# A hybrid attention layer on one core: the first loads on two queues, the first weight split and the table load moved forward, the loads of the first phase pinned in order, the causal mask made on chip

## The chip, the core and the metric

The kernel runs on one core of a Trainium2 chip. The metric is device microseconds of one execution, the median of several runs. A core has a matrix engine (TensorE; PE in the profile, with its weight loads as PEld), a vector engine (VectorE, DVE), an activation engine (ScalarE, ACT), a general engine (GpSimd, POOL) and a queue engine (SyncE, SP) that in this kernel issues the DMA transfers. All tensors lie in the chip's memory when the kernel starts, and the output is written back there.

## The reference, cut to what matters

One decoder layer over 512 tokens of width 1024, all in float32:

```
h    = rms_norm(x, g_norm)
proj = h @ w_in                      # one wide projection, split into head groups
o_nsa  = nsa(q, kv, gate)            # 8 heads, 2 kv heads: compressed, selected and window attention
o_pool = pool(v_p);  o_mem = cross_attention(q_m, mem)
y   = concat(o_nsa*silu(z_n), o_pool*silu(z_p), o_mem*silu(z_m))
out = x + y @ w_out
```

At 512 tokens all 8 selection blocks of 64 are selected, so the selected branch and the window branch are plain causal attention with different keys and values, and both need the same causal mask. The compressed branch first turns keys and values, in blocks of 32 tokens, into 31 compressed ones with a small network (w_cmp1, w_cmp2).

## The kernel before

Every float32 product is made in three passes on the matrix engine: each operand is split into a rounded part `hi` and a rest `lo`, and hi·hi, hi·lo and lo·hi are added up in PSUM (`mm3`, lines 333 to 339). So each weight chunk goes through the same steps: a DMA into a tile `wr` (3 buffers; lines 152 and 428/429), a copy into `wh` on ACT (`split_w`, line 158), a subtraction into `wl` (line 161, on DVE or POOL), and then the matmuls.

The first phase is the projection of x onto the keys and values of the selected and window branches (called kv here). x comes transposed, in 8 chunks `xt[k]` of 128 columns of the model width (256 KB each, line 170). The weight comes in five pieces, with 1, 1, 2, 2 and 2 chunks (256 or 512 KB each, line 152). `split_gained` (lines 327 to 331) multiplies a chunk of x by the norm's gain (`g_col`, loaded at line 165) and splits it into `act_hi` (ACT, line 330) and `act_lo` (DVE, line 331). Then come 12 matmuls for each chunk: three passes for four row tiles (line 792), 96 in all. Ahead of them run `WU` = 14 warm-up matmuls on zeros (line 177).

The factor 1/rms of the rows is applied after the projection. For it the rows of x are loaded a second time, not transposed (512 KB for each of 4 row tiles, line 799), after the constants `cst` (line 796) and the positions; `row_square` sums their squares on ACT (line 309), `row_factors` makes the factors on DVE (lines 198 to 208 and 316 to 318), and `rows_to_columns` transposes them on PE (line 324) and copies them to `rstd_t` (ACT, line 325).

Then comes a list of steps, `EARLY`, in an order written out by hand: `W_kc` loads and splits the weight of the compressed branch (two chunks of 512 KB), `ci` multiplies by it (48 matmuls into two PSUM tiles, lines 337 to 339) and scales the result by `rstd_t` (DVE, line 464), `kv0` to `kv3` finish the kv row tiles (from line 393 on), `W_g`, `W_m`, `W_q` load and split the next weights, and so on; `LATE` is a second such list. The engines' own order of instructions isn't that of the program text: a planner orders each engine's stream with a timing model, and an instruction that is "kept in program order" is held behind the one traced just before it on the same engine.

The causal mask is part of `cst`: 512 columns, 384 of zeros and 128 with the triangle. `cst` has 534 KB.

Of the kernel before, what the change touches and what calls it, by code (L numbers as in the profile page):

```python
# [20 lines left out]
T = 512  # L21
# [20 lines left out]
CST_MASK = 0  # L42
CST_CMP = 512
# [8 lines left out]
def shape_constants():  # L52
    c = np.zeros((128, CST_GAIN), np.float32)
    p = np.arange(128)
    c[:, CST_MASK + 384:CST_MASK + 512] = np.where(p[None, :] <= p[:, None], 0.0, NEG)
# [12 lines left out]
    return c  # L68
# [23 lines left out]
EARLY = "W_kc kv0 kv1 kv2 W_g kv0 ci kv1 kv3 ms mr kv3 g2 g0 g0 kv2 g1 cm g1 g3 cm W_m g2 m0 m1 W_q g3 q1 cm q1 q3 m1 q0 q2 m0 q0"  # L92
LATE = "f rg rq q2 u u q3 u u f u f f u u u f c u f u u c u f u u u f f f u u u c u u u u u u c f u u u u u u u u u u f u u u u u u f"
WU = 14
# [3 lines left out]
def layer(ctx: ExitStack, tc: tile.TileContext, x, x_t, mem, mem_t, positions, g_cols, w_in, w_cmp1, w_cmp2, cmp_pos,  # L98
# [26 lines left out]
    def ps_out():  # L125
        return pp.tile([128, 512], F32, name="pO", bufs=1)
# [19 lines left out]

    def lo_eng(spec, i):
        return nc.gpsimd if spec and spec[i % len(spec)] == "p" else nc.vector

    def load_w(src, r0, kk, c0, width, name="wr", tag=None):  # L150
        wt = wp.tile([128, kk, width], F32, name="wr", bufs=3)
        nc.sync.dma_start(wt, src[r0:r0 + kk * 128, c0:c0 + width].rearrange("(k p) e -> p k e", p=128))
        return wt

    def split_w(wt, eng=None, pin=False, dst=None):
        shape = list(wt.shape)
        hi, lo = dst or (wp.tile(shape, F32R, name=name, bufs=4) for name in ("wh", "wl"))
        i = nc.scalar.activation(hi, wt, AF.Copy)  # L158
        if pin:
            tc.keep_in_program_order(i)  # L160
        (eng or nc.vector).tensor_sub(lo, wt, hi.bitcast(F32))  # L161
        return hi, lo

    g_col = cp.tile([128, 2, KT], F32, name="g_col")
    nc.sync.dma_start(g_col, g_cols)
    xt, kv_raw = [e8([128, 4, T]) for _ in range(2)], []
    xt = [xt[k // 4][:, k % 4] for k in range(KT)]
    for k0, kk in ((0, 1), (1, 1), (2, 2), (4, 2), (6, 2)):
        for k in range(k0, k0 + kk):
            nc.sync.dma_start(xt[k], x_t[:, k])  # L170
        kv_raw.append((k0, kk, load_w(w_in, k0 * 128, kk, C_KV, 512)))

    zeros = w2k([128, 256], BF16)
    nc.vector.memset(zeros, 0.0)
    warm = ps_out()
# [6 lines left out]
    nc.vector.tensor_copy(ident_r, ident)  # L182

# [136 lines left out]
    def rows_to_columns():  # L320

        pt = ps_t()
        for t in range(NT):
            nc.tensor.transpose(pt[:, t * 128:t * 128 + 128], row_rstd[:, 0, t:t + 1].to_broadcast([128, 128]), ident)
        nc.scalar.activation(rstd_t, pt, AF.Copy)
# [7 lines left out]
    def mm3(ps, pairs):  # L333

        n = len(pairs)
        for i, (sh, sl, mh, ml) in enumerate(pairs):
            nc.tensor.matmul(ps, sh, mh, start=(i == 0), stop=False)  # L337
            nc.tensor.matmul(ps, sh, ml, start=False, stop=False)  # L338
            nc.tensor.matmul(ps, sl, mh, start=False, stop=(i == n - 1))  # L339
# [20 lines left out]
    def proj_cols(ps, parts, c0):  # L360
# [5 lines left out]
        mm3(ps, pairs)  # L366
# [219 lines left out]
    def nsa_unit(pts, t, g, h, rr):  # L586
# [13 lines left out]
        p = softmax_pair(pv, n, cs[:, CST_MASK + 512 - n:CST_MASK + 512], q_nr[:, t, h:h + 1], gate[:, t, h, 1:3])  # L600
# [230 lines left out]
    def memory_rows_step():  # L831
# [7 lines left out]
        "W_kc": load_step("kc", lambda: chunk(w_in, C_KC, 256, 4, eng=LO["kc"])),  # L839
# [126 lines left out]
```

## Time and profile before

| what | value |
|---|---|
| median of 3 runs | 301.29 us (301.27 to 301.32) |
| the profiled execution, device time | 302.29 us |
| its span, first to last instruction | 300.5 us |
| PE busy | 283.7 us, 94% of the span |
| DVE, ACT, POOL busy | 72%, 57%, 14% |
| DMA moved | 30.5 MB |

The profile is of one execution. Its device time has 1.8 us outside its span, and it is 1.0 us above the median of the runs, which are not profiled. "Busy" counts instructions in flight; matmuls overlap, so the pace of a run of matmuls is read from their start times and not from their durations.

### The profile page before, as it was taken

What the parts mean: (1) busy time and instruction counts of PE and PEld (TensorE: products, weight loads), DVE (VectorE), ACT (ScalarE), POOL (GpSimd) and SP (SyncE); (2) the same over time, 40 slices, a digit from 0 to 9 for tenths busy, and PEclk for the clock granted to TensorE, in tenths of its full rate; (3) what the DMA queues carried; (4) which work ended last, traced back from release to release, by engine and by line L of the source; (5) the groups of instructions that cost most, each with busy time, mean ns of one, the idle gap of its engine ahead of it and who ended that gap; (6) DMA issues with size and microseconds to landing.
All of it is one profiled execution on the core that took longest, in us unless ns stands there. A gap on an engine that the chain in (4) does not pass through costs nothing.

```text
span 300.5 us, 4794 instructions
## 1 busy us (share of the span) xinstructions
PE 283.7 (94%) x1630; PEld 228.0 (76%) x1630; DVE 215.8 (72%) x653; ACT 172.4 (57%) x408; POOL 43.2 (14%) x67
## 2 busy tenths in 40 slices
PE   4999799989997999999999999869999999999995
PEld 3788589968875888888787888448768777877785
DVE  1674689899547986679888699997878788752221
ACT  4563743586712665778694738674687588743000
POOL 1010131312010830000000823330000000200000
PEclk9999999999998999999999999997999999999999
DMA  6999271283620082055022050720200200120031
GB/s 197 383 410 367 63 233 51 71 274 110 188 77 2 1 212 70 2 140 143 0 69 73 0 141 2 211 69 0 73 0 0 72 0 3 70 73 0 0 142 70
DMA packets 21897, 30.51 MB, mean 102 GB/s; under 512 B 2928, under 2 KB 12528, under 8 KB 21744
## 3 DMA queue, kind: packets, MB, share of 16 engines
q1 hardware_dynamic: 21872, 30.20, 31.9%
q8 instruction: 13, 0.21, 0.3%
q14 instruction: 12, 0.10, 0.1%
HBM read 28.10 MB, written 2.10 MB: 100 GB/s over the span
## 4 chain that ended last, share of the span: by engine, by line
PE 84%; DVE 9%; ACT 4%; issue 1%; DMA 1%; SPq 0%; ACTq 0%
PE pS L339 9%; PE pS L337 9%; PE pS L338 9%; PE pS L792 8%; PE pJ L339 7%; PE pJ L337 7%; PE pJ L338 7%; PE pO L621 6%; PE pT L604 5%; PE pS L598 3%; PE pT L388 2%; DVE w L536 2%; PE pS L658 1%; ACT w L538 1%; DVE w L553 1%; PE pS L471 1%
## 5 line engine op out<-in xcount | busy, mean ns | idle before, releaser
L538 ACT ACTIVATE w<-w,sm_st 128x128 f32<-128x128 f32 (+3 forms) x64 | 35.4, 555 | 9.5 <-DVE sm_st L536 9.0
L161 DVE TENSOR_TENSOR wl<-wr,wh 128x1024 fp32r<-128x1024 f32 (+3 forms) x26 | 30.4, 1169 | 10.1 <-ACT wh L158 9.9
L536 DVE CUSTOM_DVE_ANT_0 w<-pS,cst,q_nr 128x128 f32<-128x128 f32 (+3 forms) x64 | 32.6, 545 | 6.6 <-PE pT L604 5.6
L158 ACT ACTIVATE wh<-wr 128x1024 fp32r<-128x1024 f32 (+3 forms) x31 | 31.3, 1009 | 8.1 <-DMA wr<-in_w_in 6.2
L605 ACT ACTIVATE pt<-pT 128x128 f32<-128x128 f32 (+3 forms) x64 | 25.5, 429 | 18.1 <-PE pT L604 17.7
L337 PE MATMUL pS<-wh,act_hi 128*128 128x512 f32 (+2 forms) x94 | 33.8, 363 | 1.2 <-DVE w L262 1.2
L339 PE MATMUL pS<-wh,act_lo 128*128 128x512 f32 (+2 forms) x94 | 33.9, 362 | 0.0
L338 PE MATMUL pS<-wl,act_hi 128*128 128x512 f32 (+2 forms) x94 | 33.6, 361 | 0.0
L337 PE MATMUL pJ<-act_hi,wh 128*128 128x512 f32 x72 | 28.8, 399 | 1.8 <-ACT wh L158 1.8
L339 PE MATMUL pJ<-act_hi,wl 128*128 128x512 f32 x72 | 28.7, 398 | 0.1
L338 PE MATMUL pJ<-act_lo,wh 128*128 128x512 f32 x72 | 28.6, 397 | 0.0
L604 PE MATMUL pT<-ident,w 128*128 128x128 f32 x160 | 25.6, 277 | 1.5 <-ACT pt L605 0.8
L604 PEld LDWEIGHTS pT<-ident,w 128*128 128x128 f32 x160 | 19.2, 140 | 8.3 <-ACT pt L605 2.5
L553 DVE TENSOR_SCALAR w<-w,sm_st 128x256 f32<-128x256 f32 (+2 forms) x64 | 24.7, 425 | 0.9
L161 POOL TENSOR_TENSOR wl<-wr,wh 128x1024 fp32r<-128x1024 f32 x5 | 12.0, 2399 | 82.3 <-ACT wh L158 70.5
L337 PEld LDWEIGHTS pS<-wh,act_hi 128*128 128x128 f32 x94 | 18.1, 193 | 4.0 <-DVE w L262 1.3
L338 PEld LDWEIGHTS pS<-wl,act_hi 128*128 128x128 f32 x94 | 18.1, 193 | 2.4
L339 PEld LDWEIGHTS pS<-wh,act_lo 128*128 128x128 f32 x94 | 18.0, 191 | 2.4
L621 PE MATMUL pO<-pt,v_sw 128*64 128x256 f32 x160 | 19.0, 384 | 0.0
L337 PEld LDWEIGHTS pJ<-act_hi,wh 128*128 128x128 f32 x72 | 13.6, 189 | 4.4 <-ACT wh L158 2.0
L339 PEld LDWEIGHTS pJ<-act_hi,wl 128*128 128x128 f32 x72 | 13.5, 188 | 3.2 <-DVE wl L161 0.5
L338 PEld LDWEIGHTS pJ<-act_lo,wh 128*128 128x128 f32 x72 | 13.5, 188 | 2.6
(249 smaller groups left out, 631.4 us busy)
## 6 DMA issues: line engine op xcount, KB each, us to landing
wr<-in_w_in SPq DMA_DIRECT2D x15, 512.0 KB, 5.2
wr<-in_w_in SPq DMA_DIRECT2D x11, 256.0 KB, 3.8
e<-in_x_t SPq DMA_DIRECT2D x8, 256.0 KB, 7.5
e<-in_x SPq DMA_DIRECT2D x4, 512.0 KB, 8.0
wr<-in_w_mem_kv SPq DMA_DIRECT2D x4, 512.0 KB, 4.1
wr<-in_w_out SPq DMA_DIRECT2D x4, 512.0 KB, 4.0
wr<-in_w_out SPq DMA_DIRECT2D x8, 256.0 KB, 3.9
w<-in_x SPq DMA_DIRECT2D x8, 256.0 KB, 3.1
```

Of the source, the lines that this page charges most:

```text
L158: i = nc.scalar.activation(hi, wt, AF.Copy)
L161: (eng or nc.vector).tensor_sub(lo, wt, hi.bitcast(F32))
L337: nc.tensor.matmul(ps, sh, mh, start=(i == 0), stop=False)
L338: nc.tensor.matmul(ps, sh, ml, start=False, stop=False)
L339: nc.tensor.matmul(ps, sl, mh, start=False, stop=(i == n - 1))
L536: nc.vector.tensor_tensor_reduce(p[:, b, :n], ps[b], mask, r, 3e38, OP.add, OP.min, st[:, 0, b:b + 1])
L538: nc.scalar.activation(p[:, b, :n], p[:, b, :n], AF.Exp, bias=st[:, 0, b:b + 1], scale=-1.0, accum_out=st[:, 1, b:b + 1])
L553: nc.vector.tensor_scalar(p[:, b, :n], p[:, b, :n], st[:, 2, b:b + 1], None, op0=OP.mult)
L604: nc.tensor.transpose(pt[:, kt * 128:kt * 128 + 128], p[:, b, kt * 128:kt * 128 + 128], ident)
L605: nc.scalar.activation(pts[b][:, :, g, rr, :], pt[:, 0:n].rearrange("p (k q) -> p k q", k=t + 1), AF.Copy)
L621: m = nc.tensor.matmul(dst, v, p, start=(rp == 0 and i < 2), stop=(rp == 1 and i >= len(calls) - 2), skip_group_check=True)
L792: nc.tensor.matmul(kv_ps[t], a[:, k, t * 128:(t + 1) * 128], b[:, j], start=(k == 0 and b is wh and a is act_hi), stop=(k == KT - 1 and a ...
```

## The change

It moves and adds these things:

- The first weight piece and then `g_col` are issued from ACT's DMA queue; all other loads stay on SP, and SP begins with the first chunk of x.
- The loads of the first phase (x, weights, `W_kc`, `cst`, positions, rows of x, the compression weights, the memory rows) are kept in program order.
- A copy of one column of zeros on ACT is traced ahead of the first real ACT work, so the load of ACT's table comes with it.
- `wh` of the first weight piece is made by a copy on DVE.
- `WU` goes from 14 to 19.
- The two chunks of `W_kc` are loaded right after the kv weights, ahead of `cst` and the rows of x. The first is split after the kv splits, the second after the row sums.
- In `EARLY`, `ci` stands right behind `W_kc`; the first matmul of each of its two groups is kept in program order, and `rows_to_columns` is done between the two groups.
- The mask is made by POOL (a memset of 512 columns and one affine select on 128), and `cst` loses 512 columns (256 KB).

```diff
-EARLY = "W_kc kv0 kv1 kv2 W_g kv0 ci kv1 kv3 ms mr ...
+EARLY = "W_kc ci kv0 kv1 kv2 W_g kv0 kv1 kv3 ms mr ...
-WU = 14
+WU = 19
...
-    def split_w(wt, eng=None, pin=False, dst=None):
+    def split_w(wt, eng=None, pin=False, dst=None, hi_eng=None):
...
+        if hi_eng is not None:
+            hi_eng.tensor_copy(hi, wt)
+        else:
+            i = nc.scalar.activation(hi, wt, AF.Copy)
+            if pin:
+                tc.keep_in_program_order(i)
         (eng or nc.vector).tensor_sub(lo, wt, hi.bitcast(F32))
...
     g_col = cp.tile([128, 2, KT], F32, name="g_col")
-    nc.sync.dma_start(g_col, g_cols)
...
         for k in range(k0, k0 + kk):
-            nc.sync.dma_start(xt[k], x_t[:, k])
-        kv_raw.append((k0, kk, load_w(w_in, k0 * 128, kk, C_KV, 512)))
+            pinned(nc.sync.dma_start(xt[k], x_t[:, k]))
+        if k0 == 0:
+            wt = wp.tile([128, 1, 512], F32, name="wr", bufs=3)
+            nc.scalar.dma_start(wt, w_in[0:128, C_KV:C_KV + 512].rearrange("(k p) e -> p k e", p=128))
+            nc.scalar.dma_start(g_col, g_cols)
+        else:
+            wt = load_w(w_in, k0 * 128, kk, C_KV, 512, pin=True)
+        kv_raw.append((k0, kk, wt))
...
     nc.vector.memset(zeros, 0.0)
+    nc.scalar.activation(kp.tile([128, 1], F32, name="act0", bufs=1), zeros[:, 0:1], AF.Copy)
...
+    causal = cp.tile([128, T], F32, name="causal")
+    nc.gpsimd.memset(causal, 0.0)
+    nc.gpsimd.affine_select(out=causal[:, T - 128:], in_=causal[:, T - 128:], pattern=[[-1, 128]],
+                            compare_op=OP.is_ge, fill=NEG, base=0, channel_multiplier=1)
...
     def compress_in(kv2, parts):
         for i in range(2):
             ps = ps_early()
-            proj_cols(ps, parts, i * 128)
+            proj_cols(ps, parts, i * 128, pin=True)
+            if i == 0:
+                rows_to_columns()
...
-        wh, wl = split_w(wt)
+        wh, wl = split_w(wt, hi_eng=nc.vector if k0 == 0 else None)
...
+    kc_raw = [load_w(w_in, k0 * 128, 4, C_KC, 256, pin=True) for k0 in (0, 4)]
+    kc_parts = [(0, 4) + split_w(kc_raw[0], pin=True)]
...
-    nc.sync.dma_start(cs, cst)
-    nc.sync.dma_start(pos_i, positions)
+    pinned(nc.sync.dma_start(cs, cst))
+    pinned(nc.sync.dma_start(pos_i, positions))
     for t in range(NT):
-        nc.sync.dma_start(xs[t], x_rows[t])
+        pinned(nc.sync.dma_start(xs[t], x_rows[t]))
         row_square(xs[t], t)
+    kc_parts.append((4, 4) + split_w(kc_raw[1], pin=True))
     row_factors(0, NT)
-    rows_to_columns()
...
-        "W_kc": load_step("kc", lambda: chunk(w_in, C_KC, 256, 4, eng=LO["kc"])),
+        "W_kc": load_step("kc", lambda: kc_parts),
```

## Rows read from the trace of the kernel before

**Rows 1.** The chain that ended last, its beginning: start us, us, what.
```profile
0.73 0.38 SPq L165
1.17 3.14 DMA e<-in_x_t
4.38 1.28 ACT L330
5.67 0.72 ACT act_hi L330
6.39 0.53 ACT wh L158
6.97 24.11 PE pS L792 x93
...
32.94 0.95 ACT wh L158
```
**Rows 2.** Timeline, PE: start us, us, engine line op out<-in, [idle before <-releaser].
```profile
1.05 3.17 PE L177 MATMUL pO<-w 128*128 128x256 bf16 x14 [1.05 <-DVE w L174]
...
8.84 1.91 PE L792 MATMUL pS<-wl,act_hi 128*128 128x512 f32 x4
...
10.54 1.91 PE L792 MATMUL pS<-wh,act_lo 128*128 128x512 f32 x4
...
15.26 1.07 PE L792 MATMUL pS<-wh,act_hi 128*128 128x512 f32 x4
16.16 1.07 PE L792 MATMUL pS<-wl,act_hi 128*128 128x512 f32 x4
...
31.58 0.60 PE L324 MATMUL pT<-ident,row_rstd 128*128 128x128 f32 x4
33.94 0.50 PE L337 MATMUL pJ<-act_hi,wh 128*128 128x512 f32 x1 [1.76 <-ACT wh L158]
```
**Rows 3.** Timeline, the loads and splits of the kv phase.
```profile
1.64 0.42 SPq L152 DMA_DIRECT2D wr<-in_w_in  x1
1.76 0.23 DVE L182 CAST ident_r<-ident 128x128 fp32r<-128x128 f32 x1 [0.77 <-POOL ident masks.py:199]
...
7.10 0.68 DVE L161 TENSOR_TENSOR wl<-wr,wh 128x512 fp32r<-128x512 f32 x1
...
12.42 1.06 ACT L158 ACTIVATE wh<-wr 128x1024 fp32r<-128x1024 f32 x1 [0.62 <-DMA wr<-in_w_in]
13.10 3.03 SPq L799 DMA_DIRECT2D e<-in_x  x4
...
13.52 1.23 DVE L161 TENSOR_TENSOR wl<-wr,wh 128x1024 fp32r<-128x1024 f32 x1 [0.93 <-ACT wh L158]
```
**Rows 4.** Timeline, from the rows of x to the kv row tiles.
```profile
19.25 1.10 POOL L803 TENSOR_SCALAR cst<-cst 128x2 f32<-128x2 f32 x1 [17.52 <-DMA cst<-in_cst]
...
25.35 0.18 ACT L309 ACTIVATION_READ_ACCUMULATOR w<-e 128x1 f32 x1
...
28.34 0.16 DVE L316 TENSOR_SCALAR row_rstd<-row_rstd 128x4 f32<-128x4 f32 x1
...
31.10 0.47 ACT L393 ACTIVATE v_sw<-pS,row_rstd 128x256 f32<-128x256 f32 x1 [5.56 <-PE pS L792]
```
**Rows 5.** DMA issues of 10 to 20 us: what, KB each, median us from issue to landing.
```profile
e<-in_x SPq DMA_DIRECT2D x4, 512.0 KB, 8.0
```
**Rows 6.** Windows: stretch, us, busy (and count) of each engine, granted clock, DMA share, GB/s.
```profile
30.00:35.00 5.00, 3.24 (x16) 2.28 (x14) 2.86 (x13) 3.90 (x8) 0.00 (x0) 1.00 0.21 65
...
45.00:55.00 10.00, 10.00 (x77) 9.76 (x77) 9.51 (x27) 3.83 (x8) 1.50 (x6) 1.00 0.21 69
...
65.00:70.00 5.00, 4.33 (x20) 3.38 (x21) 5.00 (x19) 3.87 (x11) 0.00 (x0) 1.00 0.83 314
...
90.00:95.00 5.00, 2.78 (x15) 2.06 (x15) 3.16 (x17) 1.61 (x6) 0.64 (x1) 0.97 0.01 3
95.00:100.00 5.00, 5.00 (x17) 3.88 (x17) 4.53 (x16) 1.49 (x3) 1.51 (x4) 0.69 0.00 0
```

More of the change, by code (lines that the diff above doesn't have):

```diff
@@ L40 @@
 C_GATE, C_ZN, C_VP, C_ZP, C_QM, C_ZM = 1280, 1304, 1816, 2072, 2328, 2584
-CST_MASK = 0
-CST_CMP = 512
+CST_CMP = 0
 CST_PCNT = CST_CMP + NT * 32
@@ L54, in shape_constants @@
     p = np.arange(128)
-    c[:, CST_MASK + 384:CST_MASK + 512] = np.where(p[None, :] <= p[:, None], 0.0, NEG)
     n = np.arange(32)
@@ L91 @@
 PF = ('aa', 'vv', 'vv', 'vv')
-EARLY = "W_kc kv0 kv1 kv2 W_g kv0 ci kv1 kv3 ms mr kv3 g2 g0 g0 kv2 g1 cm g1 g3 cm W_m g2 m0 m1 W_q g3 q1 cm q1 q3 m1 q0 q2 m0 q0"
+EARLY = "W_kc ci kv0 kv1 kv2 W_g kv0 kv1 kv3 ms mr kv3 g2 g0 g0 kv2 g1 cm g1 g3 cm W_m g2 m0 m1 W_q g3 q1 cm q1 q3 m1 q0 q2 m0 q0"
 LATE = "f rg rq q2 u u q3 u u f u f f u u u f c u f u u c u f u u u f f f u u u c u u u u u u c f u u u u u u u u u u f u u u u u u f"
-WU = 14
+WU = 19
 @with_exitstack
@@ L145, in e4, with load_w @@
         return ep.tile(shape, dtype, name="e4", bufs=2)
+    pinned = tc.keep_in_program_order
     def lo_eng(spec, i):
         return nc.gpsimd if spec and spec[i % len(spec)] == "p" else nc.vector
-    def load_w(src, r0, kk, c0, width, name="wr", tag=None):
+    def load_w(src, r0, kk, c0, width, pin=False):
         wt = wp.tile([128, kk, width], F32, name="wr", bufs=3)
-        nc.sync.dma_start(wt, src[r0:r0 + kk * 128, c0:c0 + width].rearrange("(k p) e -> p k e", p=128))
+        i = nc.sync.dma_start(wt, src[r0:r0 + kk * 128, c0:c0 + width].rearrange("(k p) e -> p k e", p=128))
+        if pin:
+            tc.keep_in_program_order(i)
         return wt
-    def split_w(wt, eng=None, pin=False, dst=None):
+    def split_w(wt, eng=None, pin=False, dst=None, hi_eng=None):
         shape = list(wt.shape)
         hi, lo = dst or (wp.tile(shape, F32R, name=name, bufs=4) for name in ("wh", "wl"))
-        i = nc.scalar.activation(hi, wt, AF.Copy)
-        if pin:
-            tc.keep_in_program_order(i)
+        if hi_eng is not None:
+            hi_eng.tensor_copy(hi, wt)
+        else:
+            i = nc.scalar.activation(hi, wt, AF.Copy)
+            if pin:
+                tc.keep_in_program_order(i)
         (eng or nc.vector).tensor_sub(lo, wt, hi.bitcast(F32))
@@ L323, in rows_to_columns @@
         for t in range(NT):
-            nc.tensor.transpose(pt[:, t * 128:t * 128 + 128], row_rstd[:, 0, t:t + 1].to_broadcast([128, 128]), ident)
+            pinned(nc.tensor.transpose(pt[:, t * 128:t * 128 + 128], row_rstd[:, 0, t:t + 1].to_broadcast([128, 128]),
+                                       ident))
         nc.scalar.activation(rstd_t, pt, AF.Copy)
@@ L331, in split_gained, with mm3 @@
         nc.vector.scalar_tensor_tensor(lo, src, g, hi.bitcast(F32), op0=OP.mult, op1=OP.subtract)
-    def mm3(ps, pairs):
+    def mm3(ps, pairs, pin=False):
         n = len(pairs)
         for i, (sh, sl, mh, ml) in enumerate(pairs):
-            nc.tensor.matmul(ps, sh, mh, start=(i == 0), stop=False)
+            first = nc.tensor.matmul(ps, sh, mh, start=(i == 0), stop=False)
+            if pin and i == 0:
+                pinned(first)
             nc.tensor.matmul(ps, sh, ml, start=False, stop=False)
@@ L358, in proj_rows, with proj_cols @@
         mm3(ps, pairs)
-    def proj_cols(ps, parts, c0):
+    def proj_cols(ps, parts, c0, pin=False):
         pairs = []
@@ L365, in proj_cols @@
                               act_hi[:, k0 + j, :], act_lo[:, k0 + j, :]))
-        mm3(ps, pairs)
+        mm3(ps, pairs, pin)
     q_st = sp.tile([128, H, T], F32R, name="q_st")
@@ L450, in compress_loads @@
     def compress_loads(kv2, w1):
-        nc.sync.dma_start(w1, w_cmp1)
-        nc.sync.dma_start(w2, w_cmp2)
-        nc.sync.dma_start(pe, cmp_pos)
+        for dst, src in ((w1, w_cmp1), (w2, w_cmp2), (pe, cmp_pos)):
+            pinned(nc.sync.dma_start(dst, src))
         nc.gpsimd.tensor_copy(kv2[:, :, :, T - 16:T], pe.unsqueeze(2).to_broadcast([128, 2, G, CMP_STRIDE]))
@@ L599, in nsa_unit @@
                                      start=(i == 0), stop=(i == 1))
-        p = softmax_pair(pv, n, cs[:, CST_MASK + 512 - n:CST_MASK + 512], q_nr[:, t, h:h + 1], gate[:, t, h, 1:3])
+        p = softmax_pair(pv, n, causal[:, T - n:], q_nr[:, t, h:h + 1], gate[:, t, h, 1:3])
         for b in range(2):
@@ L810, in mem_scale_step @@
             mx = e4([128, D])
-            nc.sync.dma_start(mx, mem_rows[t])
+            pinned(nc.sync.dma_start(mx, mem_rows[t]))
             row_square(mx, NT + t)
```

## The prediction

> **What bounds the kernel now.** I read the chain of work that ended last first, since the change is at the start, then the timeline along it, then tables by stage for the time behind it. The chain begins with the load of x's first chunk, goes through the table load, one activation and one weight copy on ACT, and then stays on PE for 24.11 us [rows 1]. So PE is the bound from 6.97 us on, and ahead of it stands a string of work in which PE waits. In the timeline of PE [rows 2] the reader should look at start times. Four kv matmuls begin at 8.84 and the next four at 10.54, 425 ns apiece; later the starts are 15.26 and 16.16, 226 ns apiece. The granted clock reads 1.00 in the rows of the profile here all the same, so the pace alone shows that the first ones run at the lower level, 1.2 GHz. The 96 matmuls take from 6.97 to 31.58, 24.6 us, where 96 at 226.5 ns would take 21.75: 2.86 us go to the lower clock. Then four transposes, 0.6 us, and PE stands idle for 1.76 us until `wh` of `W_kc` is made [rows 2]. That copy starts on ACT only at 32.94 [rows 1], behind the copies of the kv tiles that begin at 31.10 [rows 4]. These two places, up to 6.97 us and around 32 us, are what the change touches. Further on DVE is nearly full (9.51 of 10 us from 45 to 55, 5.00 of 5 from 65 to 70, where PE idles 0.67), and PE idles 2.2 us between 90 and 95 with a granted clock of 0.69 in the 5 us after it [rows 6].
>
> **First loads.** SP's issues stand 0.44 to 0.47 us apart (0.73, 1.17, 1.64) [rows 1, 3]. Without `g_col` in front x's first chunk is issued at 0.73 instead of 1.17 and lands 3.14 us later, at about 3.9. `w` of the first piece goes out on ACT at about the same time, 0.9 us sooner than now; everything behind it on SP is 0.90 us sooner (two issues fewer). Price on ACT: two issues, some 0.9 us, in time in which ACT now waits for x until 4.38 [rows 1].
>
> By the Trainium skill (DMA: Bandwidth & Descriptors, Issuing engines are not separate DMA queues) a second issuing queue brings no bandwidth, only the issue time. The trace has one queue in use and can't show it; the sum above counts only issue time, so it is the sum by this rule, and a true doubling of bandwidth would bring the third piece's landing nearer to the upper bound below.
>
> **Table load and first split.** The table load, 1.28 us, stands behind the wait for x [rows 1]; with the dummy copy it ends by about 3 (two issues until 1.6, then 1.28), ahead of x's landing. The first `wh` (0.53 us of the chain [rows 1]) goes to DVE beside `act_hi` (0.72). A DVE copy of 128x512 has no row: it lies between the 128x128 cast, 0.23, and the subtraction of 128x512, 0.68 [rows 3]; I take 0.6, nearer to the one of its size. PE's first operands are then ready at 3.9 + 0.72 = 4.6, or, if DVE puts `act_lo` (some 0.7) ahead of its copy, at 6.0.
>
> **Warm-up.** 14 warm-up matmuls take 3.17 us from 1.05 [rows 2], 0.226 each; 19 take 4.30 and end at 5.35. So PE starts the kv work at 5.35 (up to 6.0), 1.6 us sooner, and the warm-up, not the data, sets it.
>
> **The clock.** In the old trace PE worked 3.17 us, paused 2.75, and then needed from 6.97 to about 12.8 (5.8 us, from the paces above: 2.86 us lost at 0.2 us for each matmul are 14 slow ones) to come to the full pace. Now there is hardly a pause, so counted from 1.05 the rise would come at about 6.9: about 4 slow matmuls, 0.7 us lost. Bounds: 0, and 2.86 as now.
>
> **Third weight piece.** Two chunks (24 matmuls, 5.44 us) from 5.35 with 0.7 lost end at 11.5. Now chunk 2 starts at 15.26, but its `wh` was copied from 12.42 on, when its weight landed, to 13.48, and `wl` took 1.23 more [rows 3]. Sent 0.9 us sooner, the weight lands at 11.5 and `wh` is ready at 12.6. So PE waits here about a microsecond, and 0.3 more for `wl` (1.23 against four matmuls, 0.91): chunk 2 effectively starts at 12.9, 2.4 us sooner than 15.26. The four later pieces of work come faster than PE uses them up, as they do now. **Gain of the kv phase: 2.4 us**, end at 29.2. If the weight lands no sooner than now, 1.5; if PE never waits for it (11.5), 3.8. If the clock stays low as long as before, 24 matmuls end at 13.6, so the gain is 1.6: the wait for the weight hides most of that difference.
>
> **The gap at 32 us.** With `W_kc` loaded and split before, PE goes from kv straight to `ci`: the 1.76 us go. What has to cover it: chunk one waits for the third `wr` buffer to come free (now 14.75, `wl` of the third piece [rows 3]; about 13.8 then), lands some 8 us later (the median of 512 KB loads in the full queue [rows 5]), 22, and needs 1.1 + 1.2 for its splits; PE wants it at 29.2. Chunk two is some 2.7 us behind, and is wanted after 12 matmuls, at 31.9. Without this cover the old 1.76 stand. ACT's and DVE's part of it (two subtractions of 1.23) moves into a stretch where both have room. **Gain: 1.8 us.**
>
> **The rows of x go behind `W_kc`.** Their issues began at 13.10 and took 3.03 [rows 3]; the last square ended at 25.5 and the factors at 28.5 [rows 4]. Now SP must first wait for the buffer of `W_kc`'s second chunk, and stands there with `cst`, the positions, the rows and all later loads behind it: about 16 to 17, so they are issued at about 17 to 20 and land by 25 to 28. The lighter queue and 256 KB less of `cst` help. Squares and factors keep their 1.3 and 3.1 us: 29.5 to 32. PE wants them at 29.2 + 24 x 0.2265 = 34.6, where the transposes now stand between the groups of `ci`. So nothing on PE, with 2.6 us or more to spare; the kv tiles start between 1.6 us sooner and 0.9 later than 31.1.
>
> **Mask.** Two POOL instructions, where POOL idles 17.5 us until `cst` comes [rows 4]; priced at nothing, at most a row of its size there, 1.10, which that idle time covers as well.
>
> **Sum.** 2.4 + 1.8 = 4.2 us off the profiled span of 300.5: 296.3. That execution took 302.29, 1.8 outside its span; its device time is 1.0 above the median of the runs. So 301.29 - 4.2 = **297.1 us**. Bounds of the unknowns: 1.5 + 1.8 gives 298.0, 3.8 + 1.8 gives 295.7.
>
> **Rivals.**
> - *DVE takes the gain back.* Behind 30 us DVE works almost without a gap. What speaks for it is its full rows, and that the kv tiles may start no sooner than now. Against it: 2.5 us of its work (the two subtractions) are moved ahead of 29. If the start stays at 31.1, only these 2.5 us are left, minus the waits at 65 growing by up to 1.7: 298.8 to 300.5. Chance 0.2.
> - *A later stall goes as well.* The wait at 90 to 95 (2.2 us), with its clock of 0.69 for 5 us (1.55 us), and the 0.67 at 65 are chains through ACT and DVE; with other phases between the engines one of them can vanish. About 3 us more: 293 to 294.5. Against it: nothing in the change is aimed there. Chance 0.16.
> - *No gain at the kv phase's start:* DVE copies late and the clock stays low. Then the weight sets the pace and 1.5 + 1.8 is left, inside the forecast's bounds.
> - *Slower.* The transposes of the factors are kept between the groups of `ci`, so PE blocks if the factors are late. From 34.6 on each microsecond costs one; the gain is gone at 38.8, which needs the last row of x to land at 34.4 instead of 25 to 28, or at 37.2 if a clock drop like the one at 95 (1.55) follows. At 40 the time is 301.3 + 1.2 + 1.55 = 304. For it: SP stands at a wait with everything behind it. Against: such loads take about 8 us in a full queue [rows 5], which gives the 28, and 6 us are left to the point. Chance 0.08.
>
> **How the numbers follow.** The forecast has 0.52 (295.7 to 298.0, and half a microsecond around), the DVE rival 0.2, the later stall 0.16, slower 0.08, no change beyond all this 0.04. The range leaves out the slower case and the ends of the DVE rival and of the best case: 293.3 to 300.2. A measurement of this kernel tells from no change what is over 0.2%, 0.6 us. The DVE rival ends beyond 300.7 in few cases; faster 0.87, same 0.05, slower 0.08.
>
> **What would show it.** Right: kv matmuls from about 5.4 us on, chunk 2 from about 12.6, the last one ending at about 29, no idle time of PE between it and `ci`, transposes of the factors at about 34.6 without a wait, and PE's lead of 4 us still there at 60 and at 100. Wrong: a wait of PE for DVE's first copy; slow pace up to 11 us; a third piece that lands at 12.4 or that doesn't hold PE at all; a growing wait around 60 to 67; an idle stretch with a low clock where there was none.

## The result, and the profile of the changed kernel

Twenty executions of the changed kernel have a median of 299.81 us (295.25 to 302.21), twenty of the kernel before 301.33 (300.91 to 302.78). The ratio of the runs compared is 0.9869 [0.9842, 0.9896], which times 301.33 is 297.4 us: faster, and close to the 297.1 forecast. The ratio counts only executions within 1.5% of the fastest of their kernel, all twenty of before and seven of the changed kernel (295.25 to 299.64), and the profile below is of one that it leaves out (301.6 us, span 299.8), so its span isn't set against the 300.5 of before; its waits are what is read. Over all twenty the medians are only 1.5 us, 0.5%, apart. The ratios of the experiments further on are against executions of the kernel before from the same round, with medians of 301.73 to 302.47. The spread is itself part of the result. Sorted by mean granted clock, the twenty times are 295.25 to 297.27 at 1.00 (four), 299.8 at 0.994, 298.45 and 298.88 at 0.988 and 0.989, 299.64 to 301.10 at 0.977 (six), 301.34 to 302.21 at 0.972 (seven).

The chain that ended last, of the changed kernel, its beginning (start us, us, what); it answers to [rows 1]:

```profile
1.17 4.96 DMA g_col<-in_g_cols
6.22 0.73 ACT act_hi L347
7.00 23.68 PE pS L812 x96
```

x's first chunk, the table load and the first weight copy are gone from the chain, and yet PE starts at 7.00 as before (6.97). The new first link is the load of 8 KB of gain columns, which takes 4.96 us. The timeline of the same stretch (start us, us, engine line op, [idle before <-releaser]), against [rows 2, 3]:

```profile
0.73 0.41 ACTq L178 DMA_DIRECT2D wr<-in_w_in  x1
1.05 3.73 PE L189 MATMUL pO<-w 128*128 128x256 bf16 x19 [1.05 <-DVE w L185]
1.17 0.45 ACTq L179 DMA_DIRECT2D g_col<-in_g_cols  x1
1.65 1.28 ACT L186 ACT_TABLE_LOAD   x1 [1.65 <-PEq L978]
...
3.06 0.68 SPq L152 DMA_DIRECT2D wr<-in_w_in  x1
...
4.93 0.43 DVE L161 CAST wh<-wr 128x512 fp32r<-128x512 f32 x1 [2.41 <-DMA wr<-in_w_in]
...
6.22 1.34 ACT L347 ACTIVATE act_hi<-e,g_col 128x512 fp32r<-128x512 f32 x2 [3.08 <-DMA g_col<-in_g_cols]
...
7.00 1.64 PE L812 MATMUL pS<-wh,act_hi 128*128 128x512 f32 x4 [2.21 <-ACT act_hi L347]
...
8.43 1.91 PE L812 MATMUL pS<-wl,act_hi 128*128 128x512 f32 x4
...
9.39 1.06 ACT L163 ACTIVATE wh<-wr 128x1024 fp32r<-128x1024 f32 x1
10.14 1.47 PE L812 MATMUL pS<-wh,act_lo 128*128 128x512 f32 x4
...
11.44 1.09 PE L812 MATMUL pS<-wh,act_hi 128*128 128x512 f32 x4
...
14.19 1.07 PE L812 MATMUL pS<-wh,act_hi 128*128 128x512 f32 x4
```

The reader should see four things. The table load ends at 2.93, hidden, as forecast. DVE's copy of 128x512 takes 0.43 (0.6 was taken) and is done at 5.36, ahead of `act_hi`. The warm-up of 19 ends at 4.78, not 5.35: 19 in 3.73 is 0.196 each against 0.226 for the 14 of before, so its last ones already ran at the higher level; then PE waits 2.21 us, and the first kv matmuls run at the lower one (1.91 for a group of four against 1.09 later). The copy of the third weight piece, at 9.39, has no wait for its load in front, and PE none for it: chunk 2 starts at 14.19, 1.1 us sooner than before.

The timeline from the end of the kv phase, against [rows 2, 4]:

```profile
29.60 1.07 PE L812 MATMUL pS<-wh,act_lo 128*128 128x512 f32 x4
...
30.51 0.39 PE L354 MATMUL pJ<-act_hi,wh 128*128 128x512 f32 x1
...
31.02 0.47 ACT L412 ACTIVATE v_sw<-pS,row_rstd 128x256 f32<-128x256 f32 x1
...
35.95 0.60 PE L340 MATMUL pT<-ident,row_rstd 128*128 128x128 f32 x4
...
36.59 0.60 ACT L342 ACTIVATE rstd_t<-pT 128x512 f32<-128x512 f32 x1 [2.94 <-PE pT L340]
37.22 2.73 DVE L484 TENSOR_TENSOR e<-pJ,rstd_t 64x496 f32<-64x496 f32 x4 [2.35 <-ACT rstd_t L342]
...
41.69 0.42 DVE L422 TENSOR_TENSOR w<-pS,rm_st 128x256 f32<-128x256 f32 x1
```

No idle time stands between kv and `ci` at 30.51, and none before the transposes. But DVE waits 2.35 us for `rstd_t`, then evacuates the first `ci` group, and scales the first kv tile only at 41.69. In the timeline of the kernel before the same step is

```profile
36.11 0.42 DVE L403 TENSOR_TENSOR w<-pS,rm_st 128x256 f32<-128x256 f32 x1
```

The windows of the changed kernel (columns as in [rows 6]):

```profile
0.00:10.00 10.00, 6.73 (x27) 4.96 (x28) 4.60 (x9) 5.18 (x8) 1.88 (x9) 0.88 0.81 275
...
40.00:50.00 10.00, 8.91 (x65) 8.42 (x64) 8.99 (x30) 3.67 (x8) 1.70 (x5) 1.00 0.32 107
50.00:60.00 10.00, 8.18 (x74) 7.98 (x76) 9.29 (x32) 6.68 (x11) 4.38 (x11) 1.00 0.10 20
60.00:70.00 10.00, 7.54 (x73) 6.45 (x69) 9.58 (x35) 8.40 (x23) 2.62 (x5) 0.78 0.72 245
70.00:80.00 10.00, 10.00 (x44) 8.08 (x44) 3.85 (x14) 4.89 (x9) 0.00 (x0) 0.88 0.19 52
...
90.00:100.00 10.00, 10.00 (x46) 7.81 (x45) 8.43 (x28) 3.38 (x8) 4.53 (x10) 1.00 0.01 2
```

From 40 to 70 PE now idles 1.09 + 1.82 + 2.46 = 5.4 us, where before it idled 1.13, all of it in the last of these windows:

```profile
60.00:70.00 10.00, 8.87 (x83) 7.08 (x79) 9.69 (x33) 8.87 (x22) 1.41 (x4) 1.00 0.79 264
```

PE's largest waits there are these three (what waited for what: us in total, times, longest us); two more, 0.6 and 0.3 us, are of transposes at L407:

```profile
PE pS L354 <- ACT e L347: 1.6, 1, 1.6
PE pS L491 <- issue: 1.5, 1, 1.5
PE pS L354 <- DVE w L422: 1.4, 1, 1.4
```

The last of them, at 50.28, is for the scaling of a kv tile; "issue" means that the profile shows nothing that was waited for. From 90 to 100 PE has no idle time, where before it lost 2.2 us and then ran at 0.69 [rows 6]. The clock falls to 0.78 and 0.88 behind the new idle time.

**Bookkeeping.** `ci` begins at 30.51 instead of 33.94, 3.4 us sooner; 0.6 of that are the transposes, which PE now does behind the first group, so 2.8 us are gained. The idle time of 40 to 70 takes 5.4 - 1.1 = 4.3 back. The stall at 90 with its low clock (2.2 + 0.31 x 5.00 = 3.8) is gone. The low clock of 60 to 80 costs 0.22 x 7.54 + 0.12 x 10 = 2.9 in this execution. That is 2.8 - 4.3 + 3.8 - 2.9 = -0.6, where the trace shows a gain of 0.8, so 1.4 us stay unexplained: the first output matmul of memory attention starts at 145.0 instead of 145.8. From there to the end it is 154.8 us, before 154.7.

### The profile page after: what moved, and what is told of

It is laid out like the page before. It is cut to its first block, busy times and chain, and to the rows that moved or that the text cites. A ratio compares the mean times of both kernels' runs of the same rounds, so it can differ in the third digit from the quotient of the medians.

```text
span 299.8 us, 4813 instructions
## 1 busy us (share of the span) xinstructions
PE 284.3 (95%) x1635; PEld 229.6 (77%) x1635; DVE 215.2 (72%) x654; ACT 171.7 (57%) x408; POOL 43.7 (15%) x69
## 4 chain that ended last, share of the span: by engine, by line
PE 83%; DVE 9%; DMA 3%; ACT 3%; issue 1%; ACTq 0%; SPq 0%
PE pS L354 10%; PE pS L357 9%; PE pS L358 9%; PE pS L812 8%; PE pJ L354 7%; PE pJ L358 7%; PE pJ L357 7%; PE pO L641 6%; PE pT L624 5%; PE pS L618 3%; PE pT L407 2%; DVE w L556 2%; DMA e<-in_mem_t 2%; DMA g_col<-in_g_cols 2%; PE pS L678 1%; ACT w L558 1%
## 5 line engine op out<-in xcount | busy, mean ns | idle before, releaser
L163 ACT ACTIVATE wh<-wr 128x1024 fp32r<-128x1024 f32 (+3 forms) x30 | 30.6, 1019 | 16.1 <-PE pS L358 7.4
L556 DVE CUSTOM_DVE_ANT_0 w<-pS,causal,q_nr 128x128 f32<-128x128 f32 (+3 forms) x64 | 32.6, 546 | 6.7 <-PE pT L624 5.7
L358 PE MATMUL pS<-wh,act_lo 128*128 128x512 f32 (+2 forms) x94 | 33.3, 354 | 0.0
L624 PE MATMUL pT<-ident,w 128*128 128x128 f32 x160 | 26.2, 282 | 1.5 <-ACT pt L625 0.8
L624 PEld LDWEIGHTS pT<-ident,w 128*128 128x128 f32 x160 | 19.8, 144 | 8.6 <-ACT pt L625 2.5
L641 PEld LDWEIGHTS pO<-pt,v_sw 128*64 128x64 f32 x160 | 10.8, 136 | 6.1 <-issue 1.5
```

The source lines that it names most:

```text
L556: nc.vector.tensor_tensor_reduce(p[:, b, :n], ps[b], mask, r, 3e38, OP.add, OP.min, st[:, 0, b:b + 1])
L624: nc.tensor.transpose(pt[:, kt * 128:kt * 128 + 128], p[:, b, kt * 128:kt * 128 + 128], ident)
L641: m = nc.tensor.matmul(dst, v, p, start=(rp == 0 and i < 2), stop=(rp == 1 and i >= len(calls) - 2), skip_group_check=True)
```

## The experiments

Three theories stood against each other. **A**: DVE gets the factors late, because their transposes now stand behind the first `ci` group, and PE's lead is lost to it between 48 and 67 us. **B**: the gain is there in every execution, and only falls of the granted clock take it back. **C**: the planner puts the later streams into another order after any edit at the start, and that order decides. The table sums up what the traces gave. M is the start of the first output matmul of memory attention. The later order is that of PE's matmuls from the start of memory attention, some 25 us ahead of M, to the end (1032 matmuls), set against the kernel before. In e4, e5 and e6 14 more matmuls stand behind M than before, in e8 24 fewer, so in these four the time from M to the end also holds work that moved across M.

| kernel | first and last kv start | PE idle 40 to 70, 70 to 100 | M | M to end of span | PE's later order |
|---|---|---|---|---|---|
| before | 7.0, 31.4 | 1.1, 2.2 | 145.8 | 154.7 | - |
| changed | 7.0, 30.3 | 5.4, 0.0 | 145.0 | 154.8 | identical |
| e1 | 7.0, 30.3 | 5.3, 0.0 | 144.9 | 154.9 | identical |
| e2 | 7.5, 31.7 | 5.3, 0.0 | 145.7 | 155.3 | nearly identical |
| e3 | 7.2, 30.5 | 1.3, 1.9 | 141.6 | 154.7 | identical |
| e4 | 7.5, 30.8 | 4.1, 0.0 | 146.7 | 161.1 | another |
| e5 | 5.2, 28.3 | 0.0, 0.0 | 139.8 | 161.7 | another |
| e6 | 7.7, 29.3 | 4.2, 0.9 | 142.8 | 158.2 | another |
| e7 | 7.0, 30.0 | 4.0, 0.0 | 142.5 | 153.1 | nearly identical |
| e8 | 7.0, 31.0 | 6.0, 0.5 | 150.3 | 151.1 | another |
| e9 | 5.4, 28.3 | 5.7, 0.0 | 142.8 | 155.9 | nearly identical |
| e10 | 7.5, 29.2 | 4.8, 0.0 | 142.0 | 153.2 | identical |
| e11 | 7.0, 30.3 | 0.0, 0.0 | 146.5 | 154.5 | nearly identical |
| e12 | 5.1, 27.4 | 2.9, 1.9 | 142.6 | 154.6 | identical |

The column of idle times shows something that the order behind M doesn't. The stretch ahead of M, from the first matmul of the compression network (at 55 to 60 us) to M, has PE's matmuls in two kinds of order, leaving aside e11 and the four kernels with another later order. In e3 and e12 98% of them stand as in the kernel before (84% do in the changed kernel): PE idles 1 to 3 us from 40 to 70 and some 2 us from 70 to 100. In e1 and e10 all, in e2, e7 and e9 96% stand as in the changed kernel: PE idles 4 to 6 us from 40 to 70 and none from 70 to 100. So theory C reaches into this stretch as well, also where the later order is identical.

**The changed kernel again (e1).** No edit.

> The changed kernel once more, to have a second profile of it and more runs. Theory A (the lead of some 4 us that PE has at 42 us is lost between 48 and 67 us because DVE gets the column factors late): the waits of PE at 48 to 50, 56 to 59 and 64 to 66 us are there again, about 5 us together, whatever the clock does. Theory B (only the granted clock takes the gain back: it falls after a pause of PE in some executions): in an execution with a mean clock near 1.00 the waits are there too but the time is some 5 us shorter than in one of 0.972. Both expect a ratio to the kernel before of 0.984 to 0.990.

Median 299.68 (295.53 to 301.55, six executions), ratio 0.9851 [0.9802, 0.9899]. The waits are those of above (2.2 at the kv start, 1.5, 1.5 and 1.4 later), and the times stand with the clock again: 295.53 and 296.92 at 1.00, 299.93 at 0.994, 299.44 and 300.95 at 0.977, 301.55 at 0.972. One kernel with one order of instructions has executions 6 us apart. That speaks for B as far as the spread goes. It doesn't make the waits of 40 to 70 go away.

**Gain columns ahead of the weight, on the same queue (e2).**

```diff
+            nc.scalar.dma_start(g_col, g_cols)
             nc.scalar.dma_start(wt, w_in[0:128, C_KV:C_KV + 512]...)
-            nc.scalar.dma_start(g_col, g_cols)
```

> One pair of lines swapped: on ACT's queue the gain columns are issued ahead of the first weight piece. Both theories: the gain lands by about 3 us instead of 6.2, so the first kv matmul starts at the end of the warm-up, near 5 us instead of 7.0, and the last one ends near 28.5 to 29 instead of 30.5. Theory A: DVE's late column factors don't depend on it, the waits between 48 and 67 us grow by most of that, and the time changes by less than 0.8 us. Theory B: the pause of 2.2 us ahead of the kv matmuls goes and with it the drop of the clock at 6 to 11 us, so the whole gain stays: 1.5 to 3 us less than the changed kernel.

Median 302.08 (298.79 to 303.91, twelve), ratio 0.9985 [0.9959, 1.0012]. The timeline of e2:

```profile
3.93 0.72 ACT L347 ACTIVATE act_hi<-e,g_col 128x512 fp32r<-128x512 f32 x1 [0.79 <-DMA g_col<-in_g_cols]
...
6.90 0.43 DVE L161 CAST wh<-wr 128x512 fp32r<-128x512 f32 x1 [1.46 <-DMA wr<-in_w_in]
7.47 2.05 PE L812 MATMUL pS<-wh,act_hi 128*128 128x512 f32 x4 [2.19 <-ACT act_hi L347]
```

The gain columns now come at 3.9, but the weight, second on ACT's queue, is there only at 6.9 instead of 4.9. PE starts later than in the changed kernel. All theories missed this. Whatever was second on that queue landed some 5 us or more after its issue at 1.17.

**The transposes of the factors back to their old place (e3).** They follow the factors and are free of program order.

```diff
-            if i == 0:
-                rows_to_columns()
...
     row_factors(0, NT)
+    rows_to_columns()
```

> The transposes of the row factors are put back behind the row factors, not pinned, as in the kernel before; all else is the changed kernel. Theory A: the copy of the column factors is ready by about 34 instead of 37.2 us, DVE's wait of 2.3 us for it goes, the first kv row tile is scaled by about 37 instead of 41.7, and the waits of PE between 48 and 67 us shrink by 2 us or more; the time falls by 1.5 to 4 us. Theory B: no change of the waits beyond 0.5 us, time within 0.5 us of the changed kernel in executions of the same clock.

Median 297.69 (296.67 to 301.94, six), ratio 0.9838 [0.9813, 0.9863]. The timeline and one window of e3:

```profile
31.92 0.62 PE L340 MATMUL pT<-ident,row_rstd 128*128 128x128 f32 x4 [1.04 <-DVE row_rstd L224]
...
37.02 0.42 DVE L421 TENSOR_TENSOR w<-pS,rm_st 128x256 f32<-128x256 f32 x1
...
39.01 2.72 DVE L481 TENSOR_TENSOR e<-pJ,rstd_t 64x496 f32<-64x496 f32 x4
```

```profile
60.00:70.00 10.00, 8.69 (x58) 6.80 (x55) 8.92 (x30) 7.05 (x18) 0.00 (x0) 1.00 0.52 163
```

PE pays 1.04 us at 31 for factors that aren't ready. For it DVE no longer waits for `rstd_t` and scales the first kv tile at 37.02, ahead of the evacuation, 4.7 us sooner than in the changed kernel. PE's idle time from 40 to 70 falls from 5.4 to the 1.3 of this window, and M comes 3.4 us sooner with the later order identical. That is what A expected, but it doesn't show A's reason. Idle time of 1.9 us between 80 and 100 (1.04 and 0.85 in the two windows) comes back in exchange, so from 30 us to M PE idles 4.2 us instead of 5.4: 1.1 us of the 3.4. The low clock of the changed kernel's profile from 60 to 80, priced at 2.9 above, is missing in e3 (1.00 there) and would cover the rest. And with the edit the planner also put PE's work ahead of M into another order, nearly that of before; no run moves the transposes alone. The ratio's interval overlaps with that of the changed kernel. In executions of like mean clock (0.988 to 0.994, four each) e3 took 296.67 to 298.10 us and the changed kernel, with e1, 298.45 to 299.93: that speaks for a gain, from few executions.

**Each part of the change alone (e7, e8).** e7 is the kernel before with ACT's two issues, the early table load, the copy on DVE, 19 warm-ups and the loads of x kept in program order; its diff to the kernel before follows in part. e8 is the changed kernel with the same lines taken away again and `g_col` first on SP.

```diff
-WU = 14
+WU = 19
...
+            nc.scalar.dma_start(wt, w_in[0:128, C_KV:C_KV + 512]...)
+            nc.scalar.dma_start(g_col, g_cols)
...
+    nc.scalar.activation(kp.tile([128, 1], F32, name="act0", bufs=1), zeros[:, 0:1], AF.Copy)
...
+        wh, wl = split_w(wt, hi_eng=nc.vector if k0 == 0 else None)
```

> The kernel before with the first part of the change alone: first weight piece and gain columns on ACT's queue, table load ahead, first weight copy on DVE, 19 warm-ups. The early load of the compressed branch's weight, the moved step, the moved transposes and the mask stay as before. Theory A: kv starts at 7.0 and ends near 30.5, a microsecond sooner than before, and the gap of 1.8 us behind it stays: 0.3% to 0.4% faster than before, no wait of PE between 48 and 60. Theory C: not foreseen, 0.98 to 1.02.

> The changed kernel with its first part taken back: gain columns and all loads on SP, no early table load, first weight copy on ACT, 14 warm-ups. Theory A: kv runs from 7.0 to 31.4 as before, the compressed branch's matmuls follow without a gap (1.8 us sooner than before), the column factors are late as in the changed kernel, and PE waits 2 us or more between 48 and 67: between 0.3% faster and 0.3% slower than before. Theory C: not foreseen, 0.98 to 1.02.

e7: median 299.48 (297.44 to 301.75, nine), ratio 0.9926 [0.9889, 0.9963]. Its kv phase starts at 7.02 at the low pace, like that of the changed kernel, and the gap at 30 is 0.67 instead of 1.76. Theory A expected no wait of PE between 48 and 60 here, since neither the transposes nor `ci` were moved; DVE scales the first kv tile at 34.56, sooner than before, and waits for no `rstd_t`. But PE idles 4.0 us from 40 to 70. The windows and the largest waits of e7:

```profile
50.00:60.00 10.00, 8.50 (x85) 8.30 (x85) 9.27 (x33) 7.46 (x14) 4.63 (x11) 1.00 0.28 93
60.00:70.00 10.00, 7.47 (x73) 6.30 (x69) 9.58 (x36) 8.37 (x22) 2.10 (x5) 1.00 0.66 220
```

```profile
PE pS L344 <- ACT e L337: 1.6, 1, 1.6
PE pS L478 <- issue: 1.5, 1, 1.5
```

These are the first two waits of the changed kernel at the same size, and the two smaller ones (0.6 and 0.3) are there too. So 4.0 of its 5.4 us don't come from the late factors. What is left for A is the third, 1.4 us for the scaling of a kv tile. It is there where the first tile is scaled late, in the changed kernel (41.69), in e2 (43.15, 1.2 us) and in e9 (44.15, 1.5 us), and not in e3 (37.02), e7 (34.56) and e10 (39.71).

e8: median 303.8 (303.2 to 305.06, six), ratio 1.0073 [1.0051, 1.0095], slower and outside the 0.3% that A allowed. Its kv phase ends 0.4 us sooner than before, its PE idles 1.67 + 1.08 + 3.2 us from 40 to 70, and it has another later order. So the first part brings its 0.7% alone (medians 299.48 and 301.73), and over all its executions the whole change shows no more (0.5%): the ratios' intervals overlap, and the runs don't show that the second part adds to it. The second part loses without the first, here with a later order that differs, so the loss can't be put down to its loads and splits alone.

**The old list with the new loads (e11).** `ci` back to its place in `EARLY`.

```diff
-EARLY = "W_kc ci kv0 kv1 kv2 W_g kv0 kv1 kv3 ms mr ...
+EARLY = "W_kc kv0 kv1 kv2 W_g kv0 ci kv1 kv3 ms mr ...
```

> The changed kernel with the list of steps as before, so that the compressed branch's matmuls stand behind the first kv tiles and the next weight. The planner then puts 18 matmuls of the gate weight right behind the kv matmuls, and they need a PSUM tile that the kv row tiles free only after their DVE work. All theories: PE waits there from 30.5 to about 37, 5 to 7 us, and the factors' transposes come later by as much; late order nearly the same. 1 to 5 us slower than the changed kernel, so 0.99 to 1.005 of the kernel before.

Median 302.75 (300.96 to 304.22, twelve), ratio 1.0015 [0.9993, 1.0037]. PE's longest wait in e11 (what waited for what: us in total, times, longest us):

```profile
PE pS L354 <- DVE w L422: 7.4, 1, 7.4
```

With the old list the first work behind the kv phase isn't `ci` but a projection that waits 7.42 us for DVE's scaling of a kv tile. So the new loads and splits alone bring nothing here: what they are worth hangs on `ci` being the work that PE does while DVE gets to the kv tiles.

**Gain columns first on SP, factors back; and both with ACT's queue as in e2 (e5, e4).**

The diff of e5, to which the edit of e3 comes; e4 has the edits of e2 and e3.

```diff
+    pinned(nc.sync.dma_start(g_col, g_cols))
...
-            nc.scalar.dma_start(g_col, g_cols)
```

> The gain columns are issued first on SP, as in the kernel before, so that the first weight piece is alone at the head of ACT's queue, and the transposes of the factors are put back. Theory A (what is issued second on ACT's queue lands 5 to 6 us after its issue; the late column factors make DVE late): both operands are there at 5.0 to 5.4, the first kv matmul starts by 5.5, the last one ends near 28, and the waits between 48 and 67 us stay under 2 us: 2 to 3 us less than with the transposes put back alone, so 294 to 296. Theory C (what counts is the order in which the planner then puts the engines' streams, and any edit of the start reshuffles it): kv starts at 5.5 too, but the time can lie anywhere from 294 to 304, with PE's waits at other places than in the other kernels.

> Both edits of the last two kernels together. Theory A: the kv phase's 1.7 us are now kept as well, so it is 3 to 5 us faster than the changed kernel. Theory B: as the swap alone, 1.5 to 3 us faster.

e5: median 303.47 (301.36 to 306.08, twelve), ratio 1.0045 [1.0022, 1.0068]. e4: 308.54 (304.72 to 309.57, six), 1.0158 [1.0109, 1.0207]. Both are slower than before. The start of e5 is what the prediction described: the weight's copy at 3.72, kv from 5.22 at full pace, M at 139.8, the earliest of all. But from M on it takes 161.7 us, 7 more than the kernel before. Its waits there are of a kind that the changed kernel lacks or has under 1 us:

```profile
PE pJ L353 <- DVE w L735: 2.4, 1, 2.4
PE pT L621 <- DVE w L570: 1.9, 1, 1.9
PE pJ L757 <- DVE z_p L758: 1.6, 1, 1.6
```

The three add up to 5.9 us, but waits of before are missing in their place: behind M PE idles 11.25 us in all, where before it idled 7.83. That is 3.4 of the 7 us; 14 matmuls that stood ahead of M are another part, and the rest isn't accounted for. PE's later order is another one in both. This is C: an edit of the first 35 us made the planner arrange the next 250 otherwise. M came 6.0 us sooner than before, and at the end of the span all of that is gone (301.5 us, before 300.5).

**Warm-ups up to the data (e6, e10).**

```diff
-WU = 19
+WU = 34
```

e6 has 38 in this line.

> 38 warm-up matmuls instead of 19; all else is the changed kernel. The warm-up ends near 7 us, where the kv matmuls start anyway. Theory B (the clock): without the pause of 2.2 us the kv matmuls run at the full pace from 7.0 on, the last one ends near 29.0 instead of 30.5, and the time falls by 1.5 to 2.5 us. Theory A: the kv phase ends 1.5 us sooner too, but the waits of PE between 48 and 67 us grow by that much, and the time stays within 0.8 us. Theory C: the waits stand elsewhere and the time is not foreseen.

> 34 warm-up matmuls instead of 19, a number with which the planner leaves PE's late order as it was. Theory B: the warm-up ends at 6.5 to 7, the pause ahead of the kv matmuls goes, kv runs at the full pace from 7.0 and ends near 29 instead of 30.3; 1 to 2.5 us faster than the changed kernel, mean clocks of 0.98 and more. Theory A: the kv phase ends sooner too, but the waits between 48 and 67 us take most of it: within 0.8 us. Theory C: whatever is gained by the start of the memory attention stays, as the late order is the same: 154 to 156 us from its first output matmul to the end.

e6: median 302.09 (301.16 to 305.63, twelve), ratio 1.0021 [0.9994, 1.0048], with another later order (158.2 us from M on, and a wait of 4.2 us that the changed kernel has at 1.5). e10: 297.12 (296.73 to 299.67, six), ratio 0.9853 [0.9822, 0.9884], with the identical order. The timeline of e10:

```profile
1.05 6.70 PE L189 MATMUL pO<-w 128*128 128x256 bf16 x34 [1.05 <-DVE w L185]
...
7.51 1.18 PE L812 MATMUL pS<-wh,act_hi 128*128 128x512 f32 x4
...
8.52 1.08 PE L812 MATMUL pS<-wl,act_hi 128*128 128x512 f32 x4
```

The warm-up reaches to the data, PE starts 0.5 us later than in the changed kernel, and at full pace from the first group on: the last kv matmul starts 1.1 us sooner (29.2 for 30.3). Its median over all its runs is the lowest of all kernels, 2.7 us under the changed one. By their ratios the two can't be told apart (0.9853 and 0.9869 with overlapping intervals), though none of e10's six executions takes over 299.67 us and thirteen of the changed kernel's twenty do; six executions (0.994 four times, 0.977 twice) are too few to say that the clock falls less often. The edits of e3 and e10 were not tried together.

**Gain columns first on SP, alone (e9, e12).** e9 is the changed kernel with this and `WU` 21; e12 is e7 with the first two edits.

```diff
+    pinned(nc.sync.dma_start(g_col, g_cols))
...
-            nc.scalar.dma_start(g_col, g_cols)
...
-WU = 19
+WU = 21
```

> The changed kernel with the gain columns first on SP (so the first weight piece is alone at the head of ACT's queue) and 21 warm-ups instead of 19, a number with which the planner keeps nearly the changed kernel's order of PE from the memory attention on. Theory C (a kernel keeps what its start gains only if the planner's late order stays that of the kernel before): kv from 5.3 to 28.3, the transposes of the factors at 33.8, memory attention 2 us or more sooner than in the changed kernel, and from its first output matmul to the end 154 to 156 us as before: 293.5 to 296.5 in all. Theory A (DVE late): the column factors come 2 us sooner, so DVE's wait for them is under 0.5 us and PE's waits between 48 and 67 us shrink by 1 to 2 us; same total. Theory B (clock): no pause of over 1 us ahead of the kv matmuls, so the pace is full from the start; the executions with a mean clock of 0.972 become rare.

> The kernel before with the first part of the change alone, and the gain columns first on SP instead of second on ACT's queue. PE's late order is exactly that of the kernel before. Theory C: kv from 5.3 to 28.3; the factors are ready at about 28.5 as in the kernel before, the gap behind the kv matmuls is 1.5 to 3 us; 3 us sooner than the kernel before at the memory attention and 154 to 156 us from its first output matmul to the end: 296 to 298.5. Theory A: the start's gain is partly lost in waits for DVE between 45 and 67 us: 297.5 to 300. Theory B: full pace from the start, mean clock 0.985 or more in all executions.

e9: median 300.69 (297.85 to 302.19, twelve), ratio 0.9952 [0.9927, 0.9977]. e12: 299.93 (297.05 to 301.16, seven), ratio 0.9909 [0.9872, 0.9946]. Both are slower than C expected (293.5 to 296.5, and 296 to 298.5), though their later orders are nearly or wholly that of before, and one of e12's executions has a mean clock of 0.977, under B's 0.985. The timeline of e9:

```profile
3.48 0.43 DVE L161 CAST wh<-wr 128x512 fp32r<-128x512 f32 x1 [0.96 <-DMA wr<-in_w_in]
...
5.36 1.20 PE L812 MATMUL pS<-wh,act_hi 128*128 128x512 f32 x4 [0.30 <-ACT act_hi L347]
...
11.70 1.20 PE L812 MATMUL pS<-wh,act_hi 128*128 128x512 f32 x4 [0.59 <-ACT wh L163]
...
35.41 2.72 DVE L484 TENSOR_TENSOR e<-pJ,rstd_t 64x496 f32<-64x496 f32 x4
...
40.06 2.73 DVE L484 TENSOR_TENSOR e<-pO,rstd_t 64x496 f32<-64x496 f32 x4 [0.42 <-PE pO L358]
...
44.15 0.42 DVE L422 TENSOR_TENSOR w<-pS,rm_st 128x256 f32<-128x256 f32 x1
```

Here the start is near the predicted one: kv from 5.36, though it is x's activation that sets it and not the warm-up (0.30 us of wait), and the third weight piece holds PE (0.59 us; 1.3 was forecast). The last kv matmul starts 2.0 us sooner than in the changed kernel, and PE idles 1.50 + 1.50 + 2.68 = 5.7 us from 40 to 70. Both `ci` groups now come to DVE ahead of the first kv tile, which is scaled at 44.15, later still than 41.69, though DVE waits for no `rstd_t` any more. That narrows A's part: the 1.5 us that PE waits for this scaling go with the evacuations that stand ahead of the kv tiles in DVE's queue, and not with the wait of 2.35 alone. The other 4.2 us are again the waits that e7 has. In e12, without the second part of the change, the old gap is there as in the trace of before:

```profile
30.02 0.50 PE L344 MATMUL pJ<-act_hi,wh 128*128 128x512 f32 x1 [1.76 <-ACT wh L161]
```

It is the same 1.76 us to a hundredth, 3.9 us sooner. M is 3.2 us sooner than before, and the later part takes the same 154.6.

## Why the prediction came out as it did

The total came out near the forecast in the executions that the ratio counts (297.4 for 297.1); over all twenty the gain is 1.5 us, for 4.2. Several terms behind it were wrong, and that they cancelled was luck. Of the prediction's five signs of being wrong four came: the slow pace up to 11 us, a third piece that doesn't hold PE, a growing wait around 60 to 67, and a new idle stretch with a low clock.

- **First loads, wrong.** "lands 3.14 us later, at about 3.9" for x's first chunk, and "the warm-up, not the data, sets it": the start was set by `g_col`, which the prediction counted only as an issue on ACT. Issued at 1.17, it kept PE from starting until 7.00 instead of 5.35. e2 shows that the place on the queue does it (the weight is late in its stead), e5, e9 and e12 that the start is at 5.1 to 5.4 without it. Why a second load there lands so late, no run shows.
- **Table load and first split, right**: both hidden; DVE's copy takes 0.43 where 0.6 was taken.
- **The clock, mis-sized.** 0.7 us were forecast for a pause that hardly exists. With the pause of 2.2 us the kv phase took 23.5 us where 96 x 0.2265 = 21.75, so 1.8 us went. e10 and e9 have no such pause, and their groups of four take full pace from the second on.
- **Third weight piece, wrong for this kernel.** It was to hold PE until 12.9; with PE starting 1.65 us later and the piece ready for its copy at 9.39 or sooner, it held nothing. In e9, where the start was near the forecast, it did hold PE, 0.59 us. The copy starts 3.0 us sooner than in the trace of before [rows 3], the issue is 0.9 sooner (3.06 for 4.00). The rule of the Trainium skill (DMA: Bandwidth & Descriptors, Issuing engines are not separate DMA queues), that a second issuing engine saves only issue time, would give 0.9; the trace shows 2.1 more. But e8, with all its loads on SP and this piece issued at 4.01 as before, starts the same copy at 11.32, 1.1 us sooner than before without a second queue. By the windows of 2 us up to 8, 1.95 MB had moved instead of 1.60; e9, which has the weight on ACT's queue too, moved 1.67. So no run shows that the second queue brings more than the issue time.
- **Gain of the kv phase, mis-sized**: 31.58 - 30.51 = 1.07, for 2.4.
- **The gap, right**: 1.76 forecast as 1.8 and gone; `ci` starts 3.4 us sooner, of which 0.6 are the transposes moved behind it, so PE's lead is 2.8, for 4.2 forecast; what lacks is the kv phase's. e12 shows the gap intact where the second part is missing (in e7 0.67 us of it are left), e11 that loading and splitting `W_kc` sooner brings nothing when `ci` doesn't follow.
- **Rows of x and factors, right**: transposes at 35.95 without a wait, the kv tiles from 31.02. The slower rival had no wait to live on. But the step stopped at PE: who waits for the transposes on DVE, 2.35 us with the kv tiles behind it in its queue, wasn't asked. It cost PE 1.4 us at 50.28.
- **What the DVE rival and the later-stall rival foresaw came at once**: 4.3 us taken back from 40 to 70, 3.8 given at 90 to 100. Each was given as a way in which the whole would end; together they nearly cancel, which is why the likeliest case's total stood. The DVE rival's reason holds for a part only: of the 5.4 us of waits, the trace names DVE for 1.6. The rest and the vanished stall go with the order of PE's work between the compression and M, which the prediction didn't consider: kernels with the order of before keep the stall (1.9 us in e3 and e12), those with the changed kernel's order don't have it (e7, e9, e10). From 30 us to M PE idles 5.4 us now and idled 5.2 before.
- **Not in the prediction: the spread.** Executions of the changed kernel lie from 295.25 to 302.21. A range of 293.3 to 300.2 holds the compared 297.4 and not every execution.

Open is what decides whether the clock falls in an execution: the changed kernel's executions at 1.00 have no profile. Open is also why PE waits longer from 40 to 70 in that order: e10 has the same order and ends its kv phase 1.1 us sooner, and idles 4.8 us there. Open too is how much of e8's loss is the planner's order, since no run has its loads with the old order.

## What to carry to other kernels

Ask of every small load what it stands behind on its queue and who needs it first; a size of 8 KB says nothing about its landing. Before crediting a local edit, compare the order of everything that a planner arranges later, from the edit on and not only at the end: here a reshuffled part took back what the best start had given (6.0 us at M in e5). Before giving a wait to a cause, look for the same wait in a kernel that lacks the cause: e7 has three quarters of what was put down to the moved transposes. And follow a moved step to the queue of the engine that evacuates it: PE had no wait where the transposes went, and waited 1.4 us some fourteen microseconds on, because DVE took the evacuation ahead of the kv tiles.

## What the runs showed of the hardware

- The second load on ACT's queue landed late whichever it was: 8 KB issued at 1.17 were there 4.96 us later, and a 256 KB weight issued at that place in e2 was split at 6.90. As the first load on that queue, the same weight was split at 4.93 with `g_col` behind it, and at 3.48 to 3.72 with `g_col` first on SP (e5, e9, e12 at 3.60).
- The granted clock of the rows reads 1.00 in e2's first 10 us, where a group of four matmuls takes 2.05 and 1.91, and 0.88 in the changed kernel's. In these traces the pace, not that column, tells the level of the first microseconds.
- With the same kernel and the same order, executions differed by 6 to 7 us with the mean granted clock (0.972 to 1.00). In the profile of the changed kernel the falls at 7 and at 66 us stand right behind idle times of PE of 2.21 and 1.56 us; in that of e7 idle times of 1.50 and 1.61 us at 57 and 64 us are followed by 1.00.
